# Attention visits: scores issued ahead of the preceding visit's weighted sums, and the causal mask added to the kept row F

## The chip, the cores and the metric

The kernel runs on one core of a Trainium2 chip. The metric is the device time of one execution in microseconds; the time of the kernel before is the median of three runs. One execution was also taken by the hardware profiler, and the rows shown come from it. Engines are named as in the profile: PE is TensorE's matrix multiplication, PEld its loading of weights, DVE is VectorE, ACT is ScalarE, POOL is GpSimd, SP is SyncE, which here only issues transfers.

## The reference

The reference is one decoder layer over a sequence of 1024 positions with 1024 channels, in float32. A combined projection feeds two branches, a Mamba-2 scan and an attention with forgetting; sigmoid gates merge them, and an output projection with a norm follows. The change lies in the attention, which has 16 heads of 64 channels:

```python
def _forgetting_attention(q, k, v, log_f):
    seqlen = q.shape[2]
    scale = ATT_HEAD_DIM ** -0.5
    fcum = jnp.cumsum(log_f, axis=-1)
    outs = []
    for blk in range(seqlen // ATT_BLOCK):          # blocks of 128 queries
        q0, q1 = blk * ATT_BLOCK, (blk + 1) * ATT_BLOCK
        s = jnp.einsum('bhqd,bhkd->bhqk', q[:, :, q0:q1], k[:, :, :q1]).astype(jnp.float32) * scale
        s = s + fcum[:, :, q0:q1, None] - fcum[:, :, None, :q1]
        qpos = q0 + jnp.arange(ATT_BLOCK)
        kpos = jnp.arange(q1)
        s = jnp.where(kpos[None, :] <= qpos[:, None], s, -jnp.inf)
        prob = jax.nn.softmax(s, axis=-1)
        outs.append(jnp.einsum('bhqk,bhkd->bhqd', prob.astype(v.dtype), v[:, :, :q1]))
    return jnp.concatenate(outs, axis=2)
```

## The kernel before

All products of float32 matrices with weights go through one long stream. A weight matrix pair is multiplied by a seven-product scheme: the steps numbered 1 to 7 add into PSUM banks called b, c, d and e (tiles pb, pc, pd), and each operand is split into a high and a low part (the tile wop on the weights' side, x0h, x0l and so on for the activations). `stream.half()` issues half a step, six matmuls of 128x512 on PE, with the splits of later steps, the evictions of PSUM and a few "chores" beside it: loads, differences and stores which a later stage needs. ACT and DVE make each split between them (L351, L352), ACT evicts a partial product (tile s, L404), DVE adds or subtracts the next one (L414, L416, L418).

Every stage of the kernel has its own work and fills the rest of PE with stream halves. The attention stage handles two heads at once (a head pair hp, eight of them, NK), and for each head pair six visits, written m = 6 hp + g. A visit of `GROUPS` is two blocks of 128 queries (the pair, u = 0 and 1) against one half h of the keys:

```python
GROUPS = [((7, 6), 1), ((7, 6), 0), ((5, 4), 1), ((5, 4), 0), ((3, 2), 0), ((1, 0), 0)]
```

So visits g = 0, 2, 4 and 5 contain diagonal blocks, with 512 and 384 keys (g = 0 and 4) or 256 and 128 (g = 2 and 5); g = 1 and 3 are full. A visit has these parts.

- `scores`: for each of its two blocks, three matmuls of split operands for each of the two heads, on the upper and lower 64 rows of the array, into PSUM tiles s (tag "s", four banks). On a diagonal block, four more small matmuls add a triangle of 1e30 to the last 128 columns: bf16 constants `eye` and `far`, joined in the list `corner`. Then a custom DVE operation (L1467) adds the row F of the keys (tile fb, one row for each head, the same in all partitions) to the scores and takes the minimum nm, and ACT takes the exponential into the tile ex (L1471), with its sum. Queries are stored with a factor of -1/8, so the scores are negated and the mask is positive: it raises what must vanish, since the exponential is taken of the negative. These are issued with high priority and pinned in program order.
- `turned`: PE transposes ex block by block into PSUM tiles pt, which use the same four banks as s; ACT or DVE evicts each to a tile p (L1502, L1500).
- `weighted`: PE multiplies p with the values v into the PSUM tile av, one bank.
- After visits g = 1, 3 and 5 a part of the queries is finished: `settle` and `scale` make the factors on DVE and ACT, `turn` and `send` transpose and store them (ns, st), `take` loads them spread over the partitions (rb), `free` multiplies av with the gate into o (L1419), and `out` multiplies by rb, stores the result from POOL's queue, and hands it to the second phase as differences (L1539, L1548, L1549, L1563).

The order of instructions on PE is the order of the program. In a visit it is: the weighted sums of the visit before, the scores, stream halves (`fill(m, 0)`), the transposes, stream halves (`fill(m, 1)`). `rooms` and `weights` say how many halves: three and one in most visits of head pairs 0 to 3 and 6, two and one elsewhere, fewer beside the small visits. On ACT, DVE and POOL a planner orders what is not pinned, by its own costs; `tc.high_priority()` puts an instruction ahead of others. `loads(m)` issues the transfers of later visits from SP in program order. fb, k and v have one buffer for each half of the keys: those of the upper half for the next head pair are loaded after visit g = 2, those of the lower half after g = 5. POOL executes its queue in order: subtractions of the chores (L213), stores (L195, L1533, L1063) and, late in the stage, sums of weights (L357, L373).

Of the kernel before, what the change touches and what calls it, by code (L numbers as in the profile page):

```python
# [16 lines left out]
P = 128  # L17
T = 1024
D = 1024
NK = D // P  # L20
# [66 lines left out]
def hybrid_layer(ctx: ExitStack, tc, a, out):  # L87
# [1207 lines left out]
    with tc.tile_pool(name="att", bufs=1, reuse_waits="tile", side="right") as ap, tc.tile_pool(  # L1295
# [4 lines left out]
        eye = ap.tile([P, 192], BF16, name="eye")  # L1300
        far = ap.tile([P, 192], BF16, name="far")
        nc.vector.memset(eye, 0.0)
        big, beyond = small("big"), small("beyond")
        nc.vector.memset(big[:, 0:192], -NEG)
        for e in range(2):
            nc.vector.tensor_copy(eye[rows[e], 64:P], ident[rows[e], rows[e]])
            nc.gpsimd.affine_select(
                beyond[:, 192 * e : 192 * e + 192], big[:, 0:192], [[1, 192]], ALU.is_gt, 0.0, base=64 * e - 64,
                channel_multiplier=-1,
            )  # L1310
            nc.vector.tensor_copy(far[rows[e], :], beyond[rows[e], 192 * e : 192 * e + 192])

        corner = [(eye[:, 64:192], far[:, 64:192]), (eye[:, 0:P], far[:, 0:P])]
# [15 lines left out]
        def load_k(hp, h):  # L1329

            t = k[hp, h] = ap.tile([P, 2, HALF], F32R, tag=f"k{h}", name="k")
            for n, dram in enumerate((kh_dram, kl_dram)):
                nc.sync.dma_start(t[:, n, :].bitcast(F32), dram[hp, :, half(h)])
            f = fb[hp, h] = ap.tile([P, 2, HALF], F32, tag=f"fb{h}", name="fb")
            nc.sync.dma_start(f, f_dram[2 * hp : 2 * hp + 2, half(h)].unsqueeze(0).to_broadcast([P, 2, HALF]))

# [101 lines left out]
        def scores(hp, g, u):  # L1438
# [8 lines left out]
            diagonal = h == i // 4  # L1447
            for m, (x, y) in enumerate(ops):
                for e in range(2):
                    mm(  # L1450
                        s[e][:, 0:w], x[rows[e]], y[rows[e]], start=(m == 0), stop=(m == 2 and not diagonal),
                        skip_group_check=True,
                    )
            if diagonal:
                for n, (x, y) in enumerate(corner):
                    for e in range(2):
                        mm(
                            s[e][:, w - P : w], x[rows[e]], y[rows[e]], start=False, stop=(n == 1),
                            skip_group_check=True,
                        )  # L1460
            hd = heads[hp]
            for e in range(2):
# [109 lines left out]
        def loads(m):  # L1572

            hp, g = divmod(m, 6)
            more = hp + 1 < NK
            if g == 0:
                if hp:
                    load_v(hp, 0)
                if not m:

                    for j in range(KH):
                        stream.line += ops_s.differences(j, difference_tile, small)
# [31 lines left out]
        for _ in range(14):  # L1614
            stream.half()

        weights = (1.1, 1.1, 1.1, 1.1, 0.75, 0.95, 1.05, 0.85)

        rooms = [(0.8, 0.35), (0.8, 0.35), (0.55, 0.25), (0.8, 0.35), (0.75, 0.35), (0.5, 0.25)]
        left = [sum(map(sum, rooms)) * sum(weights)]  # L1620

        def fill(m, part):
            share = weights[min(m // 6, NK - 1)] * rooms[m % 6][part]
            to = stream.steps.index((ends[4], 6))
            stream.halves(round((2 * (to - stream.at) - (stream.run is not None)) * share / left[0]))
            left[0] -= share

        made = []
        for m in range(6 * NK + 1):

            for one in made:
# [7 lines left out]
            hp, g = divmod(m, 6)  # L1639
            if not g:  # L1640
                heads[hp] = Heads(hp)
            for u in range(2):
                scores(hp, g, u)
# [9 lines left out]
            fill(m, 0)  # L1653
# [14 lines left out]
            fill(m, 1)  # L1668
# [61 lines left out]
```

## Time and profile before

| | before |
|---|---|
| median of 3 runs | 1298.28 us (1296.61 to 1303.51) |
| profiled execution, own time | 1295.2 us |
| its span, first to last instruction | 1293.5 us |
| granted TensorE clock, mean | 0.998 |
| PE busy, share of the span | 1252.5 us, 97% |
| DVE busy | 1002.0 us, 77% |
| ACT busy | 790.5 us, 61% |
| POOL busy | 259.9 us, 20% |

In a row of the timeline the first number is the start from the beginning of the span and the second the time until its last instruction ends; then come the engine, the line, the operation, "out<-in" by the program's names, the shape and the count, and in brackets how long the engine had been idle and what released it. Rows of a group by line give the least, median and largest duration in ns, the first and last start, and the shapes. A row of waits gives who waited for whom, the sum in us, how many times and the longest. Matmuls are pipelined, so their durations overlap: the time that one takes of PE is read from start to next start. The line L130 is that of a helper that issues every matmul, L133 that of every transpose.

### The profile page before, as it was taken

What the parts mean: (1) busy time and instruction counts of PE and PEld (TensorE: products, weight loads), DVE (VectorE), ACT (ScalarE), POOL (GpSimd) and SP (SyncE); (2) the same over time, 40 slices, a digit from 0 to 9 for tenths busy, and PEclk for the clock granted to TensorE, in tenths of its full rate; (3) what the DMA queues carried; (4) which work ended last, traced back from release to release, by engine and by line L of the source; (5) the groups of instructions that cost most, each with busy time, mean ns of one, the idle gap of its engine ahead of it and who ended that gap; (6) DMA issues with size and microseconds to landing.
All of it is one profiled execution on the core that took longest, in us unless ns stands there. A gap on an engine that the chain in (4) does not pass through costs nothing.

```text
span 1293.5 us, 20991 instructions
## 1 busy us (share of the span) xinstructions
PE 1252.5 (97%) x7054; PEld 981.6 (76%) x7054; DVE 1002.0 (77%) x1994; ACT 790.5 (61%) x1738; POOL 259.9 (20%) x250
## 2 busy tenths in 40 slices
PE   5999999999999999999999999999999999899997
PEld 3688888787888888888877777777667777678886
DVE  7988886987788888897776666666787667786975
ACT  7745665566565665566545566566775657653754
POOL 3000440013300330124001021120001102146052
PEclk9999999999999999999999999999999999999999
DMA  8232552546336533753375565666866668656932
GB/s 297 73 111 76 160 147 92 198 145 182 127 119 203 178 128 103 212 177 117 123 232 193 183 231 193 212 223 207 285 208 241 206 198 281 209 184 197 365 117 95
DMA packets 153515, 233.57 MB, mean 181 GB/s; under 512 B 15968, under 2 KB 61504, under 8 KB 153408
## 3 DMA queue, kind: packets, MB, share of 16 engines
q1 hardware_dynamic: 137408, 197.14, 47.9%
q10 hardware_dynamic: 11136, 19.11, 3.9%
q0 software_dynamic: 4864, 15.99, 3.2%
q8 instruction: 55, 0.90, 0.3%
q14 instruction: 52, 0.43, 0.1%
HBM read 162.99 MB, written 72.34 MB: 182 GB/s over the span
## 4 chain that ended last, share of the span: by engine, by line
PE 73%; DVE 9%; DMA 7%; ACT 6%; issue 3%; SPq 1%; ACTq 0%; DVEq 0%
PE pb L130 31%; PE pc L130 17%; PE pd L130 6%; PE av L130 5%; PE pt L133 4%; PE s L130 4%; PE yps L130 2%; ACT ex L1471 2%; DVE wop L352 2%; DMA raw<-in_wu 1%; DMA xt<-in_x 1%; PE st L130 1%; ACT wop L351 1%; DVE ex L1467 1%; DVE sum L357 1%
## 5 line engine op out<-in xcount | busy, mean ns | idle before, releaser
L1471 ACT ACTIVATE ex<-ex,nm 128x512 f32<-128x512 f32 (+1 forms) x192 | 116.0, 606 | 126.4 <-DVE nm L1467 126.4
L352 DVE TENSOR_TENSOR wop<-sum,wop 128x512 fp32r<-128x512 f32 x180 | 136.8, 762 | 57.7 <-ACT wop L351 56.2
L351 ACT ACTIVATE wop<-sum 128x512 fp32r<-128x512 f32 x180 | 112.3, 625 | 99.5 <-DVE sum L357 48.7
L404 ACT ACTIVATE s<-pb 128x512 f32<-128x512 f32 x144 | 85.1, 591 | 89.6 <-PE pb L130 86.1
L352 DVE TENSOR_TENSOR wop<-raw,wop 128x512 fp32r<-128x512 f32 x144 | 102.1, 710 | 43.7 <-ACT wop L351 42.5
L130 PE MATMUL pc<-x3h,wop 128*128 128x512 f32 x384 | 130.2, 397 | 1.4 <-DVE th L414 1.0
L130 PE MATMUL pb<-x0h,wop 128*128 128x512 f32 x384 | 130.9, 398 | 0.0
L130 PE MATMUL pc<-x2h,wop 128*128 128x512 f32 x384 | 130.1, 398 | 0.5 <-DVE u L416 0.5
L130 PE MATMUL pb<-x6h,wop 128*128 128x512 f32 x384 | 129.2, 395 | 1.3 <-ACT s L404 1.3
L130 PE MATMUL pb<-x5h,wop 128*128 128x512 f32 x384 | 129.5, 396 | 0.7 <-ACT s L404 0.7
L130 PE MATMUL pb<-x4h,wop 128*128 128x512 f32 x384 | 129.5, 395 | 0.0
L1467 DVE CUSTOM_DVE_ANT_0 ex<-s,fb 128x512 f32<-128x512 f32 (+1 forms) x192 | 95.8, 553 | 33.5 <-PE s L130 33.5
L351 ACT ACTIVATE wop<-raw 128x512 fp32r<-128x512 f32 x144 | 89.6, 623 | 13.7 <-PE pd L130 6.2
L130 PE MATMUL pd<-x1h,wop 128*128 128x512 f32 x288 | 96.4, 394 | 0.0
L130 PEld LDWEIGHTS pc<-x3h,wop 128*128 128x128 f32 x384 | 72.1, 188 | 18.9 <-issue 1.5
L130 PEld LDWEIGHTS pc<-x2h,wop 128*128 128x128 f32 x384 | 72.1, 188 | 18.3 <-issue 2.5
L130 PEld LDWEIGHTS pb<-x5h,wop 128*128 128x128 f32 x384 | 72.1, 188 | 18.3 <-ACT s L404 1.6
L130 PEld LDWEIGHTS pb<-x6h,wop 128*128 128x128 f32 x384 | 72.2, 188 | 17.7 <-ACT s L404 1.7
L130 PEld LDWEIGHTS pb<-x0h,wop 128*128 128x128 f32 x384 | 72.2, 188 | 16.5 <-issue 1.6
L130 PEld LDWEIGHTS pb<-x4h,wop 128*128 128x128 f32 x384 | 72.1, 188 | 16.5 <-issue 1.4
L133 PE MATMUL pt<-ident,ex 128*128 128x128 f32 x576 | 75.9, 275 | 7.6 <-ACT ex L1471 7.2
L133 PEld LDWEIGHTS pt<-ident,ex 128*128 128x128 f32 x576 | 65.1, 140 | 19.4 <-ACT ex L1471 13.5
(310 smaller groups left out, 2910.5 us busy)
## 6 DMA issues: line engine op xcount, KB each, us to landing
raw<-in_wu SPq DMA_DIRECT2D x128, 256.0 KB
csb<-cs_dram SPq DMA_DIRECT2D x32, 256.0 KB
fb<-f_dram SPq DMA_DIRECT2D x16, 512.0 KB
rb<-st_dram SPq DMA_DIRECT2D x48, 128.0 KB
wd<-in_wo SPq DMA_DIRECT2D x40, 128.0 KB
xt<-in_x SPq DMA_DIRECT2D x8, 512.0 KB
gs_dram<-th ACTq DMA_DIRECT2D x16, 256.0 KB
qh_dram<-th ACTq DMA_DIRECT2D x16, 256.0 KB
```

Of the source, the lines that this page charges most:

```text
L130: return tc.keep_in_program_order(nc.tensor.matmul(*args, **kw))
L133: return tc.keep_in_program_order(nc.tensor.transpose(out_, in_, idn))
L351: nc.scalar.activation(op[:, 0], src, AF.Copy)
L352: nc.vector.tensor_tensor(op[:, 1], src, op[:, 0], ALU.subtract)
L357: self.adds.tensor_tensor(t, x, y, ALU.add)
L404: nc.scalar.activation(s, ps, AF.Copy)
L1467: nc.vector.tensor_tensor_reduce(o, s[e][:, 0:w], fb[hp, h][:, e, 0:w], 1.0, 3.0e38, ALU.add, ALU.min, nm)
L1471: pin(nc.scalar.activation(o, o, AF.Exp, scale=-1.0, bias=nm, accum_out=hd.at(hd.sm, i, h, e)))
```

## The change

The four bf16 matmuls of a diagonal block and their constants are taken out. In their place a triangle `beyond` of 1e30 above the diagonal is added in place to the kept row F, in the 128 columns of the diagonal block: the new function `corner(hp, i, engine)` works on both heads at once, a tile of 128x2x128. Later visits of the same head pair no longer read these columns, and earlier ones must have read them unmasked. For the second block of a visit (u = 1) DVE does it, with high priority, between the reductions of the two blocks; for the first block POOL does it, one visit ahead, from `loads` (g = 1, 3 and 4, and for block 7 of the next head pair in g = 4).

The order of a visit becomes: scores, weighted sums of the visit before, stream halves, transposes, stream halves. The halves of a visit are as many as before, but `room` divides them evenly where there are four (two and two); three are two and one, two are one and one.

```diff
--- before.py
+++ after.py
@@ -1297,20 +1297,10 @@
     ) as pp:
         rows = [slice(64 * e, 64 * e + 64) for e in range(2)]
-        eye = ap.tile([P, 192], BF16, name="eye")
-        far = ap.tile([P, 192], BF16, name="far")
-        nc.vector.memset(eye, 0.0)
-        big, beyond = small("big"), small("beyond")
-        nc.vector.memset(big[:, 0:192], -NEG)
-        for e in range(2):
-            nc.vector.tensor_copy(eye[rows[e], 64:P], ident[rows[e], rows[e]])
-            nc.gpsimd.affine_select(
-                beyond[:, 192 * e : 192 * e + 192], big[:, 0:192], [[1, 192]], ALU.is_gt, 0.0, base=64 * e - 64,
-                channel_multiplier=-1,
-            )
-            nc.vector.tensor_copy(far[rows[e], :], beyond[rows[e], 192 * e : 192 * e + 192])
-
-        corner = [(eye[:, 64:192], far[:, 64:192]), (eye[:, 0:P], far[:, 0:P])]
+        beyond = ap.tile([P, P], F32, name="beyond")
+        big = small("big")
+        nc.vector.memset(big[:, 0:P], -NEG)
+        nc.gpsimd.affine_select(beyond, big[:, 0:P], [[1, P]], ALU.is_gt, 0.0, base=0, channel_multiplier=-1)
@@ -1333,6 +1323,11 @@
                 nc.sync.dma_start(t[:, n, :].bitcast(F32), dram[hp, :, half(h)])
             f = fb[hp, h] = ap.tile([P, 2, HALF], F32, tag=f"fb{h}", name="fb")
             nc.sync.dma_start(f, f_dram[2 * hp : 2 * hp + 2, half(h)].unsqueeze(0).to_broadcast([P, 2, HALF]))
+
+        def corner(hp, i, engine):
+
+            f = fb[hp, i // 4][:, :, i % 4 * P : i % 4 * P + P]
+            pin(engine.tensor_tensor(f, f, beyond.unsqueeze(1).to_broadcast([P, 2, P]), ALU.add))
         def load_v(hp, h):
             v[hp, h] = ap.tile([P, 4, P], F32, tag=f"v{h}", name="v")
@@ -1444,21 +1439,15 @@
             t, keys = q[hp, pair], k[hp, h]
             isl = slice(i % 2 * P, i % 2 * P + P)
             ops = [(t[:, x, isl], keys[:, y, 0:w]) for x, y in ((0, 0), (0, 1), (1, 0))]
-            diagonal = h == i // 4
             for m, (x, y) in enumerate(ops):
                 for e in range(2):
                     mm(
-                        s[e][:, 0:w], x[rows[e]], y[rows[e]], start=(m == 0), stop=(m == 2 and not diagonal),
-                        skip_group_check=True,
+                        s[e][:, 0:w], x[rows[e]], y[rows[e]], start=(m == 0), stop=(m == 2), skip_group_check=True,
                     )
-            if diagonal:
-                for n, (x, y) in enumerate(corner):
-                    for e in range(2):
-                        mm(
-                            s[e][:, w - P : w], x[rows[e]], y[rows[e]], start=False, stop=(n == 1),
-                            skip_group_check=True,
-                        )
             hd = heads[hp]
+            if u and h == i // 4:
+                with tc.high_priority():
+                    corner(hp, i, nc.vector)
             for e in range(2):
                 o = ex[:, e, u, 0:w]
                 nm = hd.at(hd.nm, i, h, e)
@@ -1573,6 +1562,10 @@
             hp, g = divmod(m, 6)
             more = hp + 1 < NK
+            if g in (1, 3, 4):
+                corner(hp, {1: 5, 3: 3, 4: 1}[g], nc.gpsimd)
+            if g == 4 and more:
+                corner(hp + 1, 7, nc.gpsimd)
             if g == 0:
                 if hp:
                     load_v(hp, 0)
@@ -1613,21 +1606,31 @@
             load_v(0, h)
         for _ in range(14):
             stream.half()
+        corner(0, 7, nc.gpsimd)
         weights = (1.1, 1.1, 1.1, 1.1, 0.75, 0.95, 1.05, 0.85)
-        rooms = [(0.8, 0.35), (0.8, 0.35), (0.55, 0.25), (0.8, 0.35), (0.75, 0.35), (0.5, 0.25)]
-        left = [sum(map(sum, rooms)) * sum(weights)]
-
-        def fill(m, part):
-            share = weights[min(m // 6, NK - 1)] * rooms[m % 6][part]
+        rooms = [1.15, 1.15, 0.8, 1.15, 1.1, 0.75]
+        left = [sum(rooms) * sum(weights)]
+
+        def room(m):
+
+            share = weights[min(m // 6, NK - 1)] * rooms[m % 6]
             to = stream.steps.index((ends[4], 6))
-            stream.halves(round((2 * (to - stream.at) - (stream.run is not None)) * share / left[0]))
+            n = round((2 * (to - stream.at) - (stream.run is not None)) * share / left[0])
             left[0] -= share
+            behind = n // 2 if n > 3 else min(max(n - 1, 0), 1)
+            return n - behind, behind
         made = []
         for m in range(6 * NK + 1):
+            if m < 6 * NK:
+                hp, g = divmod(m, 6)
+                if not g:
+                    heads[hp] = Heads(hp)
+                for u in range(2):
+                    scores(hp, g, u)
             for one in made:
                 weighted(*one)
             for hd, which in end(m - 1):
@@ -1636,11 +1639,6 @@
                 stream.release()
                 heads[NK - 1].out(2)
                 break
-            hp, g = divmod(m, 6)
-            if not g:
-                heads[hp] = Heads(hp)
-            for u in range(2):
-                scores(hp, g, u)
             for hd, which in end(m - 2):
                 if hd.last and which:
                     hd.out(which)
@@ -1650,7 +1648,8 @@
             stream.release()
             for hd, which in end(m):
                 hd.settle(which)
-            fill(m, 0)
+            ahead, behind = room(m)
+            stream.halves(ahead)
             for hd, which in end(m):
                 hd.scale(which)
@@ -1665,7 +1664,7 @@
                 heads[hp].turn(2, tp)
                 heads[hp].send(2, tp)
             stream.hold()
-            fill(m, 1)
+            stream.halves(behind)
             for hd, which in end(m if m == 6 * NK - 1 else m - 1):
                 hd.take(which)
```

## The prediction

> **What bounds the kernel now.** I read the page first, then the busy time of each engine in three stretches of the attention stage, then the timeline of single visits, then the waits. The page says that TensorE works nearly without a break:
>
> ```profile
> span 1293.5 us, 20991 instructions
> PE 1252.5 (97%) x7054; PEld 981.6 (76%) x7054; DVE 1002.0 (77%) x1994; ACT 790.5 (61%) x1738; POOL 259.9 (20%) x250
> PE 73%; DVE 9%; DMA 7%; ACT 6%; issue 3%; SPq 1%; ACTq 0%; DVEq 0%
> ```
>
> The chain that ended last is 73% TensorE. So a matmul that goes away is worth its own time wherever TensorE has no wait, and a wait that goes away is worth at most TensorE's idle time. The attention stage runs from about 685 to 1137 us. By head pairs it has three stretches: pairs 0 to 3, the passage into the weights of the second phase, and the rest:
>
> ```profile
> core 0: us, PE busy (x) PEld busy (x) DVE busy (x) ACT busy (x) POOL busy (x), PEclk, DMA share, GB/s
> 685.00:911.00 226.00, 225.25 (x1541) 171.75 (x1540) 148.73 (x408) 140.56 (x356) 34.92 (x41) 1.00 0.62 200
> 911.00:965.00 54.00, 49.38 (x324) 35.30 (x324) 43.65 (x111) 41.49 (x104) 1.62 (x3) 1.00 0.79 268
> 965.00:1137.00 172.00, 164.50 (x1153) 120.54 (x1151) 125.56 (x342) 109.46 (x291) 22.83 (x35) 1.00 0.66 218
> ```
>
> TensorE idles 0.75 us in the first, 4.62 in the second, 7.50 in the third: 12.9 us in all. That is all that a better order of visits can win. DVE has a third of its time free in the first stretch, but only 10 of 54 us in the second.
>
> **The corner matmuls that go.** Each diagonal block ends with four bf16 matmuls. A visit with blocks of 512 and 384 keys, the small one with 256 and 128, and a visit without a diagonal:
>
> ```profile
> 685.92 0.97 PE L130 MATMUL s<-k,q 64*128 64x512 f32 x6
> 686.73 0.29 PE L130 MATMUL s<-far,eye 64*128 64x128 bf16 x4
> 686.82 0.77 PE L130 MATMUL s<-k,q 64*128 64x384 f32 x6
> 687.43 0.29 PE L130 MATMUL s<-far,eye 64*128 64x128 bf16 x4
> 687.65 0.50 PE L130 MATMUL pb<-x4h,wop 128*128 128x512 f32 x1
> ...
> 696.55 1.67 PE L130 MATMUL s<-k,q 64*128 64x512 f32 x12
> 698.15 0.50 PE L130 MATMUL pb<-x5h,wop 128*128 128x512 f32 x1
> ...
> 707.93 0.29 PE L130 MATMUL s<-far,eye 64*128 64x128 bf16 x4
> 708.02 0.53 PE L130 MATMUL s<-k,q 64*128 64x128 f32 x6
> 708.39 0.29 PE L130 MATMUL s<-far,eye 64*128 64x128 bf16 x4
> 708.61 0.50 PE L130 MATMUL pb<-x0h,wop 128*128 128x512 f32 x1
> ```
>
> The first column is the start; the durations overlap, so I count from start to next start. The corners take 0.09 + 0.22 = 0.31 us of a visit, in the small visit 0.09 + 0.22 too. There are 4 such visits in each of 8 head pairs: 32 x 0.31 = 9.9 us. Part of the last 0.22 may be the passage to another shape of matmul, which stays. Six pairs of 512 take 1.60 us (696.55 to 698.15); at the pace of a stream half (690.50 to 691.87 below, six matmuls of 512) they would take 1.37, so entry and exit cost 0.23, 0.12 each. With that kept, the lower end is 32 x 0.19 = 6.1. But a corner also makes the next scores enter anew: three pairs of 384 take 0.61 (686.82 to 687.43), where the pace gives 0.51. These 0.10 go too: the upper end is 32 x 0.41 = 13.1. The two nearly cancel, and I take 9.9. In the first stretch TensorE has no slack and half of it, 5.0 us, passes whole. In the other two it passes only if DVE lets it.
>
> **The mask that comes.** 64 in-place adds of 128x2x128 replace them, 32 on POOL (first block of a visit) and 32 on DVE (second block). Nearest rows, of the same 256 elements, and of the operations that lie beside them:
>
> ```profile
> L1432 DVE TENSOR_TENSOR zr<-o x16: 416/419/426, 724.7 to 1134.1; 128x256 f32<-128x256 f32 x16
> L893 POOL TENSOR_TENSOR new<-new,cdec x24: 603/1059/1065, 144.3 to 613.6; 128x256 f32<-128x256 f32 x24
> L352 DVE TENSOR_TENSOR wop<-sum,wop x180: 660/690/1782, 25.0 to 1274.1; 128x512 fp32r<-128x512 f32 x180
> L418 DVE TENSOR_TENSOR th<-s,pc x32: 673/682/689, 63.9 to 1116.1; 128x512 f32<-128x512 f32 x32
> ```
>
> On DVE 32 x 0.42 = 13.4 us are added to 318 busy us of these 452. This is hidden where DVE idles (77 us of 226 in the first stretch); it costs where DVE's chain of a visit is late, counted below, and 13.4 us if all of that cover were gone. On POOL an add takes 0.6 to 1.06 us, 19 to 34 us in all, on an engine with 59 busy of 452; the DVE reductions of the next visit wait for it. It has from the end of this visit's reductions to the next visit's, most of a visit of 7 to 11 us, so I count it at nothing; the price without that cover is a rival below. The rows of L352 and L418 show one more price: operations of the same size, but the one that reads SBUF twice stretches to 1.78 us, while the one that reads PSUM never passes 0.69. POOL's tensor operations lie beside the long ones. A POOL add can therefore hold up DVE's operand splits by its own 0.6 us. I take a third of the 16 adds after 911 us (3.2 us of DVE time), of which 40%, 1.3 us, reaches TensorE; the ends are 0 and 16 x 0.61 = 9.8.
>
> The Trainium skill, page "SBUF — State Buffer", section "SBUF: two separate sides", says that DVE with two SBUF inputs and GpSimd take an exclusive lock on one shared pair of ports for a whole instruction. The trace agrees, by the 1.78 us against 0.69 above.
>
> **The new order.** The build's own order of instructions shows each visit on TensorE. Before: scores, 1 to 3 stream halves, transposes, 1 half, weighted sums. After: scores, weighted sums of the visit before, 1 or 2 halves, transposes, 1 or 2 halves. The number of halves and of changes between shapes is the same, so nothing is added on TensorE. What changes is the cover of DVE's reductions and ACT's exponentials:
>
> ```profile
> 690.50 0.39 PE L130 MATMUL pc<-x1h,wop 128*128 128x512 f32 x1
> 691.87 1.69 PE L133 MATMUL pt<-ident,ex 128*128 128x128 f32 x14
> ...
> 1135.91 0.87 PE L130 MATMUL av<-p,v 128*64 128x256 f32 x8 [0.26 <-ACT p L1502]
> 1136.71 0.50 PE L130 MATMUL pb<-x4h,wop 128*128 128x512 f32 x1
> ...
> 688.76 0.69 DVE L1467 CUSTOM_DVE_ANT_0 ex<-s,fb 128x512 f32<-128x512 f32 x1
> 689.37 0.55 DVE L1467 CUSTOM_DVE_ANT_0 ex<-s,fb 128x384 f32<-128x384 f32 x1
> 689.85 0.55 DVE L1467 CUSTOM_DVE_ANT_0 ex<-s,fb 128x384 f32<-128x384 f32 x1
> 690.90 0.60 ACT L1471 ACTIVATE ex<-ex,nm 128x384 f32<-128x384 f32 x1
> ```
>
> A half is 1.37 us (690.50 to 691.87), eight weighted sums 0.80, sixteen twice that, 1.6. In the strong pairs 3 halves of cover (4.1 us) become 1.6 + 2.7; in the weak ones 2 (2.7) become 1.6 + 2.7, and 1 (1.4) becomes 3.0. Most waits on exponentials should go. What is late next is the first visit of a head pair, where the sums before it are only eight. Scores to transposes: 1.42 (1.73 less 0.31) + 0.80 + 2.74 = 4.96 us, and the second block's exponentials may come 0.4 later, 5.4. The chain there is 0.81 (first scores) + 2 x 0.61 + 2 x 0.48 (reductions) + 0.60 = 3.6, and whatever DVE has between the two blocks' reductions. In the built order the product of the freed weighted sums, the mask and one or two operand steps now stand there: at 0.61 us a step and 0.36 for the mask, 1.6 us in pairs 1 to 3 (no wait), about 2.3, 4.0, 2.8 and 3.4 in pairs 4 to 7: waits of 0.5, 2.2, 1.0 and 1.6. In five of these visits ACT has an exponential of the second block behind an eviction of the first transposes: 5 x 0.6 more. Pair 4's third visit has two splits and a difference between the blocks, 1.2 us late. Sum 9.5 us. To this comes one wait of before that no order cures, a transfer that arrives late:
>
> ```profile
> 915.73 0.98 PE L130 MATMUL s<-k,q 64*128 64x512 f32 x6
> 917.59 1.36 ACT L277 ACTIVATE x4h<-x4l 128x512 fp32r<-128x512 f32 x2 [1.91 <-DMA x4l<-t_s]
> 918.25 1.42 DVE L278 SCALAR_TENSOR_TENSOR x4l<-x4l,x4h 128x512 fp32r<-128x512 f32 x2 [0.79 <-ACT x4h L277]
> 919.59 0.68 DVE L1467 CUSTOM_DVE_ANT_0 ex<-s,fb 128x512 f32<-128x512 f32 x1
> ```
>
> The reductions start at 919.59 for scores begun at 915.7; I keep 2.0 us. So 12.9 us of idle become 11.5: 1.4 gained. The scores now wait for the PSUM banks of the last transposes, as the weighted sums waited for their evictions; the halves ahead of them are as many or one more, so I count no difference. SP's queue keeps its transfers in the same order around the visits, and the loads of F come two visits before their use.
>
> **Sum.** -9.9 - 1.4 + 1.3 = -10.0 us. The profiled execution took 1295.2 us (span 1293.5 and 1.7 around it) and becomes 1285.2; the median of the runs lies 3.1 above it, 1298.3, and becomes **1288.3**. A change of 0.5%, 6.5 us, is about what this measurement tells from none.
>
> **Rivals.** *All waits go*: if the late steps on DVE find their operands early, 9.9 + 12.9 = 22.8 us are won: 1275.5. For it speaks the first stretch, where TensorE already idles only 0.75 of 226; against it DVE's 81% in the second. Chance 0.17.
>
> *DVE becomes the bound after 911 us*: with 43.65 of 54 us busy, 16 more adds there (16 x 0.42 = 6.7 us) and the lock at its upper end (9.8 us), the corners' second half (4.9) and the 1.4 are not won, and up to 5 more are lost: 1298.3 - 5.0 = 1293.3 to 1298.3. The idle 46 us of DVE in the last stretch speak against it. The page "SBUF — State Buffer" of the Trainium skill, in the section named, would have each such meeting cost a whole instruction. Chance 0.23.
>
> *POOL's mask comes late*, on the slower side. POOL is served in order, and the masks are queued behind stores and subtractions that wait:
>
> ```profile
> POOL ms_dram L1063 <- DVE th L1062: 101.9, 13, 23.0
> POOL x L213 <- DMA th<-ys_dram: 79.3, 8, 23.1
> ```
>
> Three masks of a pair are needed one visit later. DVE waits for them in order, with every reduction, split and eviction behind it, and TensorE waits for the evictions. Against it: a long wait there is mostly POOL being early, for a result that the program places in the same visit; and after the place of a mask in the program 3.9 us remain until it is read (transposes 1.7, at least a half of 1.4, first scores 0.8). It decides once a mask lags over 3.9 us. If half of the 24 masks within visits lag by 1.5 us more, 18 us are lost: 1298.3 - 10 + 18 = 1306. Chance 0.12.
>
> *The change doesn't do what it says*: excluded for the corners, since the built order has none left; the reordering could leave the waits as they are (1298.3 - 9.9 + 1.3 = 1289.7), which lies inside the forecast.
>
> **How the numbers follow.** The forecast (gain of 6.5 to 18 us) has 0.48, the full gain 0.17, DVE's bound 0.23, the late mask 0.12. Faster by over 0.5%: 0.48 + 0.17 = 0.65, less 0.02 for forecasts that fall just short: 0.63. Within 0.5%: 0.23 + 0.02 = 0.25. Slower: 0.12. The range leaves out the lower part of the full gain and most of the late mask: 1278 to 1302.
>
> **What would show it.** Right: no corner matmuls; a visit with 512 and 384 keys at 1.4 us instead of 1.73; idle of TensorE between scores and transposes near zero in pairs 0 to 3, and found in the first visits of pairs 4 to 7; the DVE mask at 0.33 to 0.42 us; more long durations in the row of L352. Wrong: reductions that wait for POOL for microseconds, or TensorE idle over 15 us in the stage (forecast wrong on the slow side), or under 4 us (on the fast side).

## The result, and the profile after

The changed kernel takes 1305.75 us (median of 10 runs, 1301.94 to 1309.06), the kernel before 1298.03 beside it: a ratio of 1.0058, with a 95% interval of 1.0044 to 1.0072. It is 7.7 us slower, where 10 us of gain had been forecast, and lies 3.75 us above the range. The execution that was profiled took 1306.1 us itself. The page, and TensorE and the other engines in the three stretches of the stage (columns as in the prediction's table):

```profile
span 1304.4 us, 20591 instructions
PE 1252.7 (96%) x6798; PEld 982.1 (75%) x6798; DVE 1023.9 (78%) x2021; ACT 799.2 (61%) x1738; POOL 284.6 (22%) x281
...
685.00:911.00 226.00, 221.51 (x1395) 168.21 (x1395) 157.54 (x414) 143.06 (x350) 47.16 (x57) 0.99 0.60 200
911.00:965.00 54.00, 49.27 (x315) 36.36 (x312) 46.63 (x122) 43.01 (x105) 5.03 (x7) 1.00 0.83 272
965.00:1137.00 172.00, 159.53 (x1015) 118.00 (x1015) 129.69 (x340) 110.32 (x280) 30.37 (x45) 0.98 0.65 214
```

TensorE has 256 matmuls fewer (7054 to 6798), but idles 4.49, 4.73 and 12.47 us in the three stretches, 21.7 in all, where it idled 12.9; the changed stage runs on for 11 us behind the last stretch. From the first score to the last weighted sum the stage takes 462.0 us; it took 450.6. What stands after it takes 156.5, as before (157.0): the whole loss is in the stage.

The matmuls did become cheaper. In the first visit of the second head pair, scores with 512 and 384 keys take 1.41 us from start to next start, as forecast:

```profile
743.91 1.49 PE L130 MATMUL s<-k,q 64*128 64x512 f32 x12
745.32 0.87 PE L130 MATMUL av<-p,v 128*64 128x256 f32 x8
```

The time went into waits. These rows of the waits give who waited for whom, the sum in us, how often and the longest, first before, then after:

```profile
PEld pt L133 <- ACT ex L1471: 13.5, 28, 1.5
PE pt L133 <- ACT ex L1471: 7.2, 17, 1.3
```
```profile
PEld pt L133 <- ACT ex L1460: 29.1, 37, 2.7
PE pt L133 <- ACT ex L1460: 20.6, 28, 2.5
...
POOL fb L1330 <- DVE nm L1456: 57.2, 12, 7.8
```

The first two of each are the transposes that wait for exponentials (the same waits, seen on the weights' side and on the matmuls' side). The last says that GpSimd's masks wait for VectorE's reductions; a reduction waits for GpSimd once, 1.6 us, and not for a mask.

The same visit shows how such a wait comes about. By the first and the second row I mean, here and below, the two blocks of 128 queries of a visit; each has two reductions on VectorE and two exponentials on ScalarE, one for each head. First VectorE: the reductions are L1456, 512 wide for the first row and 384 for the second; the lines of their accumulators are left out.

```profile
746.15 0.68 DVE L1456 CUSTOM_DVE_ANT_0 ex<-s,fb 128x512 f32<-128x512 f32 x1
...
746.76 0.68 DVE L1456 CUSTOM_DVE_ANT_0 ex<-s,fb 128x512 f32<-128x512 f32 x1
...
747.38 0.99 DVE L373 TENSOR_TENSOR sum<-sum,raw 128x512 f32<-128x512 f32 x1
748.29 0.68 DVE L1414 TENSOR_TENSOR o<-av,zr 128x512 f32<-128x512 f32 x1
748.89 0.41 DVE L1330 TENSOR_TENSOR fb<-fb,beyond 128x256 f32<-128x256 f32 x1
749.33 0.56 DVE L1456 CUSTOM_DVE_ANT_0 ex<-s,fb 128x384 f32<-128x384 f32 x1
749.81 0.55 DVE L1456 CUSTOM_DVE_ANT_0 ex<-s,fb 128x384 f32<-128x384 f32 x1
```

The mask takes 0.41 us, but a sum (L373) and the product out of av (L1414, in `free`) stand ahead of it, between the rows. From the second reduction to the third are 2.57 us. In the kernel without a mask (below) it is 0.61:

```profile
745.45 0.69 DVE L1455 CUSTOM_DVE_ANT_0 ex<-s,fb 128x512 f32<-128x512 f32 x1
...
746.06 0.55 DVE L1455 CUSTOM_DVE_ANT_0 ex<-s,fb 128x384 f32<-128x384 f32 x1
```

Then, in the changed kernel again, ScalarE and, last, TensorE:

```profile
749.20 0.60 ACT L404 ACTIVATE s<-pb 128x512 f32<-128x512 f32 x1 [0.79 <-PE pb L130]
749.69 0.62 ACT L351 ACTIVATE wop<-raw 128x512 fp32r<-128x512 f32 x1
750.21 0.60 ACT L1460 ACTIVATE ex<-ex,nm 128x384 f32<-128x384 f32 x1
...
750.81 0.25 ACT L1388 ACTIVATE st<-pt 8x128 f32<-8x128 f32 x1
750.97 0.36 ACT L1491 ACTIVATE p<-pt 128x256 f32<-128x256 f32 x1
...
751.23 0.60 ACT L1460 ACTIVATE ex<-ex,nm 128x384 f32<-128x384 f32 x1
...
749.11 0.60 PE L133 MATMUL pt<-ident,ex 128*128 128x128 f32 x4
750.96 0.33 PE L133 MATMUL pt<-ident,ex 128*128 128x128 f32 x1 [1.25 <-ACT ex L1460]
751.97 1.20 PE L133 MATMUL pt<-ident,ex 128*128 128x128 f32 x9 [0.69 <-ACT ex L1460]
```

An eviction and a split of the stream (L404, L351) stand ahead of the second row's first exponential, and the evictions of the first transposes (L1388, L1491) ahead of its second. TensorE makes four transposes of ex at 749.11, waits for the one exponential, makes one, and waits for the other.

### The profile page after: what moved, and what is told of

Its sections match the earlier page's. It is cut to its first block, busy times and chain, and to the rows that moved or that the text cites. A ratio compares the mean times of both kernels' runs of the same rounds, so it can differ in the third digit from the quotient of the medians.

```text
span 1304.4 us, 20591 instructions
## 1 busy us (share of the span) xinstructions
PE 1252.7 (96%) x6798; PEld 982.1 (75%) x6798; DVE 1023.9 (78%) x2021; ACT 799.2 (61%) x1738; POOL 284.6 (22%) x281
## 5 line engine op out<-in xcount | busy, mean ns | idle before, releaser
L351 ACT ACTIVATE wop<-sum 128x512 fp32r<-128x512 f32 x180 | 112.5, 626 | 115.1 <-DVE sum L357 55.0
L352 DVE TENSOR_TENSOR wop<-sum,wop 128x512 fp32r<-128x512 f32 x180 | 138.4, 770 | 51.3 <-ACT wop L351 50.3
L404 ACT ACTIVATE s<-pb 128x512 f32<-128x512 f32 x144 | 85.3, 592 | 101.1 <-PE pb L130 99.1
L1456 DVE CUSTOM_DVE_ANT_0 ex<-s,fb 128x512 f32<-128x512 f32 (+1 forms) x192 | 99.0, 553 | 37.1 <-PE s L130 32.4
L352 DVE TENSOR_TENSOR wop<-raw,wop 128x512 fp32r<-128x512 f32 x144 | 102.5, 713 | 25.6 <-ACT wop L351 25.4
L351 ACT ACTIVATE wop<-raw 128x512 fp32r<-128x512 f32 x144 | 89.6, 623 | 19.3 <-PE pc L130 12.0
L133 PE MATMUL pt<-ident,ex 128*128 128x128 f32 x576 | 79.8, 279 | 21.0 <-ACT ex L1460 20.6
L130 PEld LDWEIGHTS pb<-x6h,wop 128*128 128x128 f32 x384 | 73.0, 190 | 18.7 <-issue 1.9
L130 PEld LDWEIGHTS pb<-x5h,wop 128*128 128x128 f32 x384 | 72.1, 188 | 18.9 <-ACT s L404 2.5
L130 PEld LDWEIGHTS pc<-x3h,wop 128*128 128x128 f32 x384 | 72.7, 189 | 17.8 <-issue 1.2
```

The costliest lines, as they stand in the source:

```text
L130: return tc.keep_in_program_order(nc.tensor.matmul(*args, **kw))
L133: return tc.keep_in_program_order(nc.tensor.transpose(out_, in_, idn))
L351: nc.scalar.activation(op[:, 0], src, AF.Copy)
L352: nc.vector.tensor_tensor(op[:, 1], src, op[:, 0], ALU.subtract)
L404: nc.scalar.activation(s, ps, AF.Copy)
L1456: nc.vector.tensor_tensor_reduce(o, s[e][:, 0:w], fb[hp, h][:, e, 0:w], 1.0, 3.0e38, ALU.add, ALU.min, nm)
```

## Experiments

"Stage" is the time from the first score to the last weighted sum in the profiled execution, "wait in the transposes" the sum, over all visits of the stage, of what lies between the starts of successive transposes of ex beyond their pace of 0.11 us. Both are read from the timelines.

| kernel | median us | ratio to before, 95% interval | stage | wait in the transposes |
|---|---|---|---|---|
| before | 1298.03 | 1 | 450.6 | 11.1 |
| after | 1305.75 | 1.0044 to 1.0072 | 462.0 | 29.3 |
| mask, old order | 1308.57 | 1.0051 to 1.0093 | 466.4 | 28.7 |
| new order, corner matmuls | 1291.42 | 0.9933 to 0.9961 | 446.8 | 9.3 |
| after, no mask at all | 1285.54 | 0.9891 to 0.9924 | 443.2 | 10.2 |
| after, GpSimd's masks only | 1281.90 | 0.9863 to 0.9898 | 438.0 | 9.6 |
| after, VectorE's masks only | 1304.50 | 1.0044 to 1.0080 | 459.9 | 28.6 |
| after, a free addition for VectorE's mask | 1287.07 | 0.9896 to 0.9928 | 442.6 | 11.9 |
| after, stream's work held behind in the stage | 1287.06 | 0.9886 to 0.9931 | 446.3 | 11.4 |
| the same edges, corner matmuls | 1292.15 | 0.9936 to 0.9968 | 446.8 | 4.3 |

**The two halves of the change.** First the mask with the old order (scores behind the weighted sums, `fill` as before), then the new order with the corner matmuls and without a mask.

> The mask in F, in the order of before (weighted sums ahead of the scores, stream halves as before). My theory: the loss comes from the two parts together, because the planner puts the gate product, the mask and the differences between the two blocks' reductions, which it can only do when the product is issued behind the scores. Then the mask alone wins the corner matmuls, about 9.9 us less some 2 for more work on DVE: 1288 to 1291 us against 1298. Rival A (the mask's work on DVE, or the lock against POOL, is the loss): as slow as the change or nearly, 1303 to 1307. Rival B (POOL's masks come late): slower than before too, 1301 or more, with reductions that wait for POOL.

> The new order of visits and halves, with the corner matmuls kept and no mask in F. My theory: without the mask the built order has the product behind the second block's reductions, so the first visits of head pairs wait less than in the change; the corners cost their 9.9 us; 1294 to 1299 us, about before. Rivals A and B: the same number, since there is no mask. Rival C (the order itself is bad, by the halves moved from ahead of the transposes to behind them): 1308 or more, above the change by some of the corners' 9.9.

They were 1308.57 and 1291.42 us. The order alone is faster by more than forecast; the mask alone loses 10 us although it spares the same matmuls. My theory, that the loss comes from the two parts together, fell with that: the loss was the mask's. In the run with the mask and the old order, the first visit of the second pair shows one part of the pattern, an eviction and a split ahead of the second row's exponentials on ScalarE:

```profile
747.80 0.58 ACT L404 ACTIVATE s<-pb 128x512 f32<-128x512 f32 x1
748.28 0.62 ACT L351 ACTIVATE wop<-raw 128x512 fp32r<-128x512 f32 x1
748.80 0.60 ACT L1460 ACTIVATE ex<-ex,nm 128x384 f32<-128x384 f32 x1
```

**Small repairs of the whole change.** First an order edge on the product out of av: `pin` keeps an operation in program order, so the planner can't move it ahead of the second row's reductions. Then one stream half behind the transposes instead of two:

```diff
-                    nc.vector.tensor_tensor(o, av, z, ALU.mult)
+                    pin(nc.vector.tensor_tensor(o, av, z, ALU.mult))
```

> The change with one word added: the gate product o<-av is kept in program order, so it and the differences traced behind it stand after the second block's reductions. My theory: TensorE's waits in the first visits of head pairs shrink from 0.5 to 4 us each to under 1, the lowered clock behind them goes too; 1288 to 1294 us. Rivals A, B and C: unchanged within 2 us, about 1305.

```diff
-            behind = n // 2 if n > 3 else min(max(n - 1, 0), 1)
+            behind = min(max(n - 1, 0), 1)
```

> The change with one stream half behind the transposes and the rest ahead of them, as in before (three and one instead of two and two; the visits with three or two halves stay). My theory: it gives the late chain 1.4 us more cover in the first visits of pairs 0 to 3 and 6, so 3 to 6 us better than the change: 1299 to 1303. Rival C (halves): back to before or better, under 1296. Rivals A and B: 1305, unchanged.

They were 1294.63 (ratio 0.9959 to 0.9991; just above the 1294 named) and 1299.16 (0.9996 to 1.0023). The edge is on one product alone, which now stands behind the second row's reductions, and gives 11 us back; one half more ahead of the transposes, where there were two and two, gives 6.6. That pointed at what stands between the rows, not at the mask.

**Which mask.** The additions were left out in `corner`, all of them or one engine's.

> The changed kernel without any mask: neither the corner matmuls nor the additions into F (the diagonal blocks stay unmasked). It is the order alone, less the corners. If the corner matmuls lie on TensorE's path as forecast (9.9 us), this is 1291.4 less 9.9 = 1281.5 (1279 to 1286). If what the corners gave back goes into waits, because TensorE comes to the transposes sooner and finds the exponentials as late as before, it stays at 1288 to 1292. Against the changed kernel (1305.8) the difference is the price of the additions and of all that they shift.

> The changed kernel with GpSimd's 32 additions only: the second rows' diagonal blocks stay unmasked. My theory now: the loss is the addition on VectorE between the two rows' reductions, for which the queues of VectorE and ScalarE are laid out otherwise (the product out of av ahead of the addition, copies of the first transposes ahead of the second row's exponentials). Then this is as fast as with no addition, within 2 us: 1280 to 1286. Rival: GpSimd's additions stretch VectorE's operations or come late: 1298 to 1306.

> The changed kernel with VectorE's 32 additions only: the first rows' diagonal blocks stay unmasked. My theory now: nearly the whole loss is still there, 1300 to 1306. Rival (GpSimd's additions are the loss): 1281 to 1290. If both have a share, it lies between, and the shares are read from this and the run with GpSimd's additions only.

1285.54, 1281.90 and 1304.50 us. GpSimd's 32 masks cost nothing (the run with them was the faster one by 3.6 us, for which I have no explanation beyond another built order). VectorE's 32 masks cost 19 us, more than their 32 x 0.42 = 13.4 us of busy time. In the waits of the three kernels, in this order, the loss stands in one place:

```profile
PEld pt L133 <- ACT ex L1459: 11.7, 19, 1.8
PE pt L133 <- ACT ex L1459: 7.0, 14, 1.3
```
```profile
PEld pt L133 <- ACT ex L1462: 9.7, 19, 1.1
PE pt L133 <- ACT ex L1462: 5.0, 14, 0.9
```
```profile
PEld pt L133 <- ACT ex L1462: 27.7, 35, 2.7
PE pt L133 <- ACT ex L1462: 19.6, 24, 2.5
```

**A first try at the queues, which told nothing.** The product out of av and ScalarE's copies and settling exponential got order edges, the stream's work did not.

> The changed kernel, mask complete, with an order edge on the product out of av (as in the earlier run at 1294.6) and on ScalarE's copies of the transposes, of the turned scales and on the settling exponential, so that they can't stand ahead of the second row's exponentials. If the loss is the queues' order and not the additions' own time: 1283 to 1290. If the additions' own time in the chain (0.42 us in each of 32 visits, up to 13.4 us) is the loss, or the place of the copies does not matter: 1293 to 1300.

1304.62 us. The copies went behind the exponentials, but the stream's sum stayed between the rows on VectorE and its eviction and split between the exponentials on ScalarE. It is a miss: against the 1294.63 with the product alone held, the further edges lost 10 us, and which of them did was not traced. The waits in the transposes explain little of it: 23.6 us, where that kernel has 21.8, for a stage of 458.4 against 450.2.

**The addition itself, or what it lets in.** In one kernel VectorE makes an addition of the same shape at the same place, for which nothing waits; its mask is left out:

```diff
-            pin(engine.tensor_tensor(f, f, beyond.unsqueeze(1).to_broadcast([P, 2, P]), ALU.add))
+            if engine is nc.vector:
+                ...
+                pin(engine.tensor_tensor(idle, f, f, ALU.add))
```

> The changed kernel without any mask (1285.5 before), with an addition of the same shape on VectorE in the place of the second row's mask that nothing waits for: F plus F into a tile of its own, not into F. The queues then are built as without a mask. Theory A (what the dependent addition lets in between is the loss): 1285 to 1292. Theory B (0.42 us of VectorE in the chain of each of 32 visits, by itself): 1298 to 1305.

1287.07 us. The 32 additions have the same median duration as the masks (0.419 us against 0.420) and cost 1.5 us, which the intervals do not tell from none, where the masks cost 19. The rows of that kernel, the group of the addition and then the first visit of the second pair:

```profile
L1326 DVE TENSOR_TENSOR idle<-fb x32: 411/419/1147, 688.0 to 1117.5; 128x256 bf16<-128x256 f32 x32
```
```profile
743.75 0.68 DVE L1452 CUSTOM_DVE_ANT_0 ex<-s,fb 128x512 f32<-128x512 f32 x1
...
744.37 0.71 DVE L1326 TENSOR_TENSOR idle<-fb 128x256 bf16<-128x256 f32 x1
745.00 0.55 DVE L1452 CUSTOM_DVE_ANT_0 ex<-s,fb 128x384 f32<-128x384 f32 x1
```

With nothing that depends on it, the planner puts the addition straight behind the reductions and the second row straight behind the addition: 1.25 us between second and third reduction, where the real mask had 2.57.

**The real mask with clean queues.** The stream's sums, splits and evictions (L351, L352, L357, L373, L381, L404) are given order edges while `attending` holds something, and so is the product out of av. In two kernels the edges were switched on at the first visit and never off, with the mask and, as the control, with the corner matmuls.

```diff
+    attending = []
+    def held(op):
+        return pin(op) if attending else op
...
-                nc.scalar.activation(op[:, 0], src, AF.Copy)
+                held(nc.scalar.activation(op[:, 0], src, AF.Copy))
```

> The changed kernel, mask complete, with order edges in the attention stage on the stream's sums, splits and evictions and on the product out of av, so that on VectorE only the addition stands between the two rows' reductions, and on ScalarE nothing between the four exponentials. Theory A (what the addition lets in between costs, not the addition): the loss of 1304.5 less 1285.5 = 19.0 us goes nearly whole, 1284 to 1291. Theory B (the 0.42 us of the addition and the wait around it in each of 32 visits are the loss): it stays at 1296 to 1305.

> The control to the run with the stream's sums behind: the same order edges, with the corner matmuls in TensorE and no addition (the new order alone had 1291.4). If the edges themselves are worth nothing: 1290 to 1293. If they delay the stream's weights, 1294 to 1300; if they help by themselves, under 1289, and then the gain of the run with the mask is theirs.

1318.99 and 1323.95 us: both expectations missed, for a reason outside the question. The edges, never taken off, also held the stream's work in the long last run behind the stage. TensorE's busy time there, in the kernel with the mask and the edges left on, and in the kernel below where they were taken off:

```profile
1128.00:1313.00 185.00, 158.10 (x646) 125.35 (x644) 119.44 (x166) 78.43 (x157) 62.90 (x45) 0.94 0.48 165
```
```profile
1129.00:1288.00 159.00, 150.65 (x661) 122.85 (x659) 119.49 (x170) 81.43 (x162) 64.78 (x45) 0.98 0.57 194
```

The stage itself had become shorter, 443.3 us. The next two kernels switch the edges on only for the stream's halves behind the scores of each pair's first visit:

```diff
+            if m % 6 == 0:
+                attending.append(1)
             stream.halves(ahead)
+            attending.clear()
```

> The changed kernel, mask complete, with order edges on the stream's sums, splits and evictions only in the part of the stream that stands right behind the scores of the first visit of each head pair, and on the product out of av. In these eight visits the queues are clean: only the addition between the reductions, nothing between the exponentials. Theory A: 1285 to 1293 (in e3, where the product alone was held, it was 1294.6). Theory B: 1294 to 1304. If the edges delay the stream's weights as they did over the whole stage: above its control by less than the corners' 9.9 us, wherever that lies.

> The control: the same order edges in the first visits and on the product, with the corner matmuls in TensorE and no addition. If the edges cost nothing: 1290 to 1293, as the new order alone. If they delay the stream's weights: 1294 to 1302, and the run with the mask is read against this one.

1289.83 (0.9914 to 0.9950) and 1289.87 (0.9921 to 0.9957). With the mask complete and eight visits repaired, the kernel is 16 us faster than without the edges. The control is as fast, so with these edges the mask is worth nothing against the corners. Last, the edges over the whole stage, taken off at its end:

> The changed kernel, mask complete, with the order edges on the stream's sums, splits and evictions and on the product out of av in the attention stage alone. In the run with the edges left on, the stage took 443.3 us from the first score to the last weighted sum (462.0 in the changed kernel, 450.6 before), and 186.2 us followed it where 157 follow elsewhere. Theory A: 443.3 + 157 and what lies ahead make 1284 to 1288. Theory B (the addition itself in the chain): not under 1296.

> The control: the same edges in the attention stage alone, corner matmuls in TensorE, no addition. The stage took 446.7 us with the edges left on: 1287 to 1292 here. The difference to the run with the mask is what the mask in place is worth with clean queues in both: 3 to 5 us of the 9.9 forecast.

1287.06 and 1292.15. This is the whole change, mask complete, 18.7 us faster than without the edges, and 11.3 us faster than before. The first visit of its second pair, VectorE, ScalarE and TensorE:

```profile
747.97 0.69 DVE L1461 CUSTOM_DVE_ANT_0 ex<-s,fb 128x512 f32<-128x512 f32 x1
...
748.70 0.43 DVE L1335 TENSOR_TENSOR fb<-fb,beyond 128x256 f32<-128x256 f32 x1
749.27 0.56 DVE L1461 CUSTOM_DVE_ANT_0 ex<-s,fb 128x384 f32<-128x384 f32 x1
...
749.01 0.71 ACT L1465 ACTIVATE ex<-ex,nm 128x512 f32<-128x512 f32 x1
...
749.87 0.62 ACT L1465 ACTIVATE ex<-ex,nm 128x384 f32<-128x384 f32 x1
...
750.49 0.60 ACT L1465 ACTIVATE ex<-ex,nm 128x384 f32<-128x384 f32 x1
...
751.56 1.69 PE L133 MATMUL pt<-ident,ex 128*128 128x128 f32 x14
```

1.30 us between second and third reduction, nothing between the exponentials, and fourteen transposes without a break. The mask and the small gaps around it cost 0.69 us of this chain (1.30 less 0.61), and that has room. Against the control the mask in place is worth 5.1 us. The edges by themselves bring nothing: the control takes 1292.15 us, the new order without edges 1291.42. So the gain is not a gain of the edges that any kernel would have had.

**Another way to the same end**: GpSimd's masks for the first rows, and for the second rows two matmuls of the full identity with the triangle in bf16 instead of four of half height; nothing on VectorE. GpSimd reads the same bf16 triangle there.

> Mask complete, in two ways: GpSimd's additions for the first rows (measured alone: 1281.9), and for the second rows two matmuls of the whole identity with the triangle, each 128 columns in BF16, in TensorE's order behind the scores; no addition on VectorE. Half of the corners' 9.9 us comes back: 1281.9 + 5 = 1287, 1283 to 1290. If GpSimd's part was free only because the second rows weren't masked: 1292 or more.

1289.18 us (0.9923 to 0.9959), without an order edge. It is faster than both kernels too; that it gains less than the whole change with edges (1287.06) is within the noise.

## Why the prediction was wrong

**The corner matmuls** were sized rightly where TensorE has work: 1.41 us for the scores, as forecast. What they bring to the end is less than the 9.9 taken: 5.9 us between the two kernels in the new order without an addition (1291.42 less 1285.54), and 5.1 with edges, where the mask in place is paid for. Both lie a little under the lower end given, 6.1, and near the 5.0 that were to pass whole in the first stretch.

**GpSimd's masks** were counted at nothing, and cost nothing: 1281.90 against 1285.54 us alone, and beside VectorE's masks 1305.75 against 1304.50, which is within the noise. Their group and that of VectorE's masks in the changed kernel (least, median and largest duration in ns):

```profile
L1330 POOL TENSOR_TENSOR fb<-fb,beyond x32: 719/739/1203, 677.3 to 1129.5; 128x256 f32<-128x256 f32 x32
L1330 DVE TENSOR_TENSOR fb<-fb,beyond x32: 407/420/816, 690.6 to 1139.6; 128x256 f32<-128x256 f32 x32
```

The medians are in the ranges forecast. The rival of the late mask named 1306 and the kernel took 1305.75, but by another way: with GpSimd's masks alone the kernel is the fastest of all. The rival of VectorE as the bound after 911 us is not what happened either: TensorE's idle time grew by 3.7 us in the first stretch already (0.75 to 4.49), where VectorE is busy for 157.5 of 226 us. The 1.3 us for VectorE and GpSimd in each other's way were not needed: of the splits on VectorE (L352), 30 take over 0.9 us before and 28 after, each of them beside a tensor operation of GpSimd. The Trainium skill, page "SBUF — State Buffer", section "SBUF: two separate sides", has VectorE with two inputs in SBUF and GpSimd take a lock on shared ports for a whole instruction; the trace agrees in single places (the sum at 747.38 takes 0.99 us beside a GpSimd subtraction, where the median of such operations is 0.69), but in the sum of the run with GpSimd's masks it shows no price.

**The new order** was forecast at 1.4 us; alone it brought 6.9 (ratio 0.9947). TensorE idled 0.5, 1.1 and 6.1 us in the three stretches there, and the first visits wait 3.4 us in the transposes: most of the first visits' waits that I charged to the order do not belong to it. They belong to the mask.

**The term that failed** is the 11.5 us of waits that the sum leaves in the stage: 10.3 in the first visits of the head pairs (0.5, 2.2, 1.0 and 1.6, five times 0.6 for ScalarE, and 2.0 for the late transfer in pair 4's), 1.2 in pair 4's third visit, none in the others. Measured in the transposes are 29.3 us, 18.9 in the first visits and 10.4 in the others. The 17.8 us between are about what the forecast misses in all (1305.75 less 1288.3 is 17.5). In the table, of the first visits, the start of the first reduction after the first score, the time from second to third reduction, and the wait in the transposes, in us (the 0.6 for ScalarE, which the prediction gives to no pair by name, are not in the forecast's column):

| head pair | first reduction, after | second to third, after | wait forecast | wait, after | wait, no mask | wait, free addition | wait, held in the stage |
|---|---|---|---|---|---|---|---|
| 0 | 2.88 | 1.78 | 0 | 2.63 | 2.49 | 1.64 | 3.75 |
| 1 | 2.25 | 2.57 | 0 | 2.38 | 0.06 | 0.36 | 0 |
| 2 | 1.11 | 1.65 | 0 | 0.76 | 0 | 0.03 | 0 |
| 3 | 0.99 | 2.06 | 0 | 0.55 | 0 | 0.15 | 0 |
| 4 | 1.90 | 2.27 | 2.5 | 2.37 | 0.57 | 0.82 | 0.74 |
| 5 | 1.20 | 3.95 | 2.2 | 3.46 | 0 | 0 | 0.67 |
| 6 | 1.98 | 3.35 | 1.0 | 2.38 | 0.13 | 0.46 | 0 |
| 7 | 2.84 | 3.35 | 1.6 | 4.42 | 2.76 | 3.38 | 0.90 |

In the first visits, the steps between the rows were not sized too small: 0.61 + 1.6 = 2.2 us were forecast in pairs 1 to 3, measured 2.57, 1.65 and 2.06; 2.9, 4.6, 3.4 and 4.0 in pairs 4 to 7, measured 2.27, 3.95, 3.35 and 3.35: 2.4 us less in all. What was mis-sized is what comes ahead of them. I let the first reduction start 0.81 us after the first score, when its scores are done (2.8 in pair 4, with the transfer). It starts 1.89 us after on the mean, because VectorE still has a split, a product or a difference of its own to finish; in pairs 1 to 7 that is 4.6 us in all over the forecast. And I let the second reduction follow 0.61 us behind the first. In pairs 2, 3, 4, 5 and 7 a split stands between these two as well (L352, L278 or L281), and it follows after 1.2 to 1.7 us: 4.0 us more. So the last exponentials of these seven visits come some 6.5 us later in all than forecast, and their waits are 6.0 us longer (16.3 against 10.3). The start could have been read before: in the first rows of the prediction the scores start at 685.92 and the second reduction at 688.76, so the first one at about 688.15, 2.2 us after them. The other 2.6 us are the first head pair's, which I left at nothing; its first visit has no weighted sums before it, so less cover, but it waits 2.49 us without any mask as well, so this is no part of the loss.

In the other visits I had counted on the new order to end the waits. They were 8.8 us before and are 4.2 without a mask, but 10.4 in the changed kernel, 9.2 more than the 1.2 counted.

The deeper error is of another kind. The late start is there without a mask too: in pairs 1 to 7 the second reduction starts 3.1 us after the first score there, 2.9 in the changed kernel, and it costs little as long as the second row follows at once. I saw in the built order that the product, one or two sums and an eviction stand between the rows, and charged them to the new order. They stand there with the mask in place, which depends on the reduction ahead of it while the one behind depends on the mask: in the first visits of the changed kernel the product stands between the rows in seven of eight, and an eviction, a split or both stand ahead of the second row's first exponential in six. With an addition for which nothing waits (1287.07 us) neither is so in any of the eight; a split or a sum is left between the rows in pairs 4, 6 and 7, as without an addition. With the real one and edges (1287.06) nothing but the mask stands there. Why the planner places them so was not followed in the planner itself. So the mask's price is neither its 13.4 us of VectorE, which were rightly called hidden, nor GpSimd; it is what the planner lets in beside a chain of three. Of 18.8 us between the stage after (462.0) and the one with no mask (443.2), the waits in the transposes make up as much (29.3 less 10.2 is 19.1). 12.9 of these are in the first visits; in the other visits the single steps were not followed.

The signs that the prediction named came out as follows: no corner matmuls, and 1.4 us for the scores, as said; waits in the first visits, but in pairs 0 to 3 too; no more long splits on VectorE; no reductions that wait for GpSimd for long; TensorE idle over 15 us, which had been named as the sign of a forecast wrong on the slow side. The forecast of 1288.3 is near what the change takes with clean queues, 1287.1, but that is the sum of errors of both signs and no merit of the working.

## What to carry to other kernels

An in-place operation between two steps of a pinned chain can cost what the planner lets in beside it, on its own engine and on the next one, and here that was nearly all of its price (1287.06 us with the other work held behind, 1285.54 without a mask). Read the built order around it with and without the dependence, and if other work moved in, hold that work with order edges, only in the stage that needs them. The start of a chain is read from the profile of each visit before, where its engine may still be busy, not from the moment when its operands are done. An edit whose time comes out as a rival said may still have another cause; leaving out each half of it is cheap and tells.

## What the hardware showed

Behind the wait in the visit above, TensorE worked at about half pace. The stretches before, beside and after (TensorE's granted clock is the third number from the end), and two matmuls of the slow one:

```profile
749.00:753.00 4.00, 2.06 (x17) 1.63 (x15) 2.23 (x7) 3.32 (x9) 1.15 (x1) 1.00 0.68 227
753.00:757.00 4.00, 4.00 (x13) 3.15 (x12) 0.47 (x1) 0.60 (x1) 0.00 (x0) 0.57 0.47 155
757.00:761.00 4.00, 4.00 (x32) 2.48 (x31) 2.57 (x8) 3.04 (x6) 0.00 (x0) 1.00 0.24 82
```
```profile
754.58 0.63 PE L130 MATMUL pb<-x6l,wop 128*128 128x512 f32 x1
755.01 1.05 PE L130 MATMUL pb<-x6h,wop 128*128 128x512 f32 x2
```

From start to next start a matmul takes 0.43 us instead of 0.23, seven times, and 0.37 twice at the ends, about 1.7 us on top of the 2.4 us of waiting. This came again after other waits of the stage (984, 1095 and 1144 us), some 4 us in all, but not after every one: waits of 2.4 to 2.6 us at 690, 923, 943 and 1032 us have no slow stretch behind them. The Trainium skill, page "TensorE: Matmul & The Clock Gate", section "What's actually happening", says that the clock falls to half after an idle window of about 3.4 us and comes back after as long a busy one. The trace agrees with the half pace and with the length: 0.57 over 4 us is half pace for 3.4 us. It differs in what sets it off, since TensorE had been idle for 2.3 us in two parts with a transpose between them, not for a whole such window. What sets it off here, and not after the other waits of that length, no run shows.
